# Two transformer blocks on one core: stage memory laid out from both ends of a partition, and one turn of the residual moved behind a group's last product

## The chip, the cores and the metric

One core of one Trainium2 chip. The metric is the time of one execution in microseconds (us) on the device, as the median of several runs; a lower time is better. A matrix product on TensorE multiplies a moving operand, streamed from on-chip memory (SBUF), by a stationary operand that was loaded from SBUF before, and adds into an accumulator bank (PSUM). SBUF has 128 partitions; every tile occupies the same bytes in each of them, so a tile's place is one byte offset. The offsets of this kernel run from 0 to 229376 (224 KiB).

## The reference

Two blocks on a residual `h` of 256 tokens x 1024 features, float32. Cut to its stages:

```python
# first block
z = rms_norm(x) @ w_in                       # differential attention, latent attention, two gates
x = x + rms_norm((sig(g_a) * (oa @ w_proj_a) + sig(g_b) * (ob @ w_proj_b)) @ w_o)
x = x + rms_norm((silu(n(x) @ w_gate) * (n(x) @ w_up)) @ w_down)
# second block, twice (i = 0: retention, i = 1: stick-breaking attention)
h = h + 0.5 * rms(swiglu(rms(h)))
h = h + rms(mixer(rms(h)))
h = h + 0.5 * rms(swiglu(rms(h)))
gate = sigmoid(rms(h) @ ple_w_gate[i])       # the gated embedding
e = p[i] @ ple_w_proj[i]
h = h + rms(gate * e)
```

## The kernel before

**Precision.** Each float32 matrix is split into a high and a low part of type float32r (`_hi`, `_lo`), and a product of two matrices is three products: hi by hi, hi by lo, lo by hi. `mm3` (lines 194 to 200) issues them in that order; all of them have line 197 in the profile. `mat_steps` (line 210; its products have line 214) is the other form, with the weights stationary and 256 tokens moving.

**Weights.** `chunk` (line 165) loads up to 2048 columns into `w_raw` (1 MB, one transfer on the SP queue), and splits them in pieces of 512 columns: ScalarE copies `w_hi` (line 188), VectorE subtracts for `w_lo` (line 189). There are 3 buffers of `w_raw` and 12 each of `w_hi` and `w_lo`.

**Stages.** In `tokens` (line 239) the stationary operand is a block of 128 tokens x 128 features of the stage's input, the moving operand 512 columns of weights. The input dimension is cut into groups; in each group token half b = 0 comes first, then b = 1, into separate PSUM banks. A feed-forward (`ffn`, line 612) runs six hidden blocks of gate and up this way with the stage input `x_hi`, `x_lo` stationary, turns each block's result `a` (transposes of line 628) and splits it into `a_hi`, `a_lo`, and then runs the down projection (`end_stage`, line 470) with `a_hi`, `a_lo` stationary. The mixers use the same forms with their own inputs: `oa`, `ob`, `m` in the first block, `u` for the retention's output, `o` for the stick-breaking output, `pe` for the embedding's projection.

**Stage joints.** At a stage's end `residual` (line 399) works for one token half: squares, a reciprocal root on GpSimd, and `h` is updated in two halves by VectorE (line 415). `features` (line 419) then turns the token half of `h`: eight transposes on TensorE (line 429, moving operand the identity in `kc`, stationary operand `h`), ScalarE makes `x_hi` (line 433), VectorE `x_lo` (line 435). It is called by the next stage's `tokens` as `before[b]`, ahead of that half's first products. Its transposes carry an order edge: they come, on TensorE, no earlier than the product kept in `self.turn_at`. `tokens` sets that name in every group and half at the product with `left == TURN_AT`, that is when 3 of the group's triples (9 products) are still to come. Turning half 0 thus stands among the last products of the stage before, turning half 1 among the products of half 0 in the first group. Within such edges the framework's scheduler orders the instructions of an engine by priority and by when it expects their inputs.

**The gated embedding** (`ple_gate`, line 1274) has two groups of the input dimension, 3 and 5 blocks. With two column parts that is 6 triples (18 products) per half in the first group and 10 triples (30 products) in the second. After the second group of a half follow tanh (`z`, line 1288), the product with `e` (line 1290), and `residual`. The next stage is the second layer's first feed-forward; after the second gated embedding the kernel ends.

**Memory.** All pools are stacked upwards from the start of SBUF in the order of their opening; pools that close give their place to the next. The bytes follow from the tile shapes and this order:

| pool or tile | bytes in a partition |
|---|---|
| descriptors and built-in constants | 0 to 16512 |
| `const` (with the identity `kc`), `raw` (3 x `w_raw`) | 16512 to 45024 |
| `hip` (`w_hi`), `lop` (`w_lo`) | 45024 to 69600, to 94176 |
| `act`: `h`; `x_hi`, `x_lo` (also `ob`) | 94176 to 102368; 102368 to 118752 |
| `sm`, `tmp` | 118752 to 136320 |
| first block: `oa`; `m` | 148608 to 164992; 164992 to 181376 |
| first block: `cq`, `ckv` | 194688 to 204928 |
| first feed-forward: `a_hi`, `a_lo` (22528 each) | 136320 to 181376 |
| `p_halves` (`pe`), open from here on | 136320 to 140416 |
| feed-forward ahead of each mixer: `a_hi`, `a_lo` | 140416 to 185472 |
| retention: `u_h`, `u_l` | 140416 to 173184 |
| stick-breaking: `o_h`, `o_l` | 152192 to 168576 |
| `emb` (`e`); feed-forward behind it: `a_hi`, `a_lo` | 140416 to 148608; 148608 to 193664 |

Of the kernel before, what the change touches and what calls it, by code (L numbers as in the profile page):

```python
# [10 lines left out]
F32 = mybir.dt.float32  # L11
# [7 lines left out]
P = 128  # L19
T = 256  # L20
D = 1024
KT = D // P
# [28 lines left out]
TURN_AT = 3  # L51
# [43 lines left out]
class Weights:  # L95


    def __init__(self):
        self.parts = []
# [45 lines left out]
class Build:  # L145
    def __init__(self, ctx, tc, aps):
        self.ctx, self.tc, self.nc = ctx, tc, tc.nc
        self.aps = aps
        self.plan = []
        self.at = 0  # L150
        pool = lambda name, bufs, **k: ctx.enter_context(tc.tile_pool(name=name, bufs=bufs, **k))
        self.const = pool("const", 1)
        self.raw = pool("raw", 3)
        self.hip = pool("hip", WB)
        self.lop = pool("lop", WB)
        self.act = pool("act", 1)
        self.sm = pool("sm", 2)
        self.tmp = pool("tmp", 2)
        self.psm = pool("psm", 4, space=PSUM)
        self.psa = pool("psa", 4, space=PSUM)  # L160
        self.filler, self.behind, self.late = Filler(), None, []
        self.later = None
# [73 lines left out]
        return ps  # L236


    def tokens(self, parts, X, nk, banks, groups, before=(None, None)):

        per = CHUNK // len(parts[0][2])
        for g in groups:
            at, order = {}, [(j, k) for j in range(len(parts)) for k in g]
            for i in range(0, len(order), per):
                part = order[i : i + per]
                W = self.chunk([(*parts[j][:2], k, parts[j][2]) for j, k in part])
                at.update({jk: (W, x * len(parts[0][2])) for x, jk in enumerate(part)})
            for b in range(2):  # L250
                if g is groups[0] and before[b] is not None:
                    before[b]()
                left = len(parts) * len(g)
                for j, (*_, cols) in enumerate(parts):
                    for k in g:
                        left -= 1
                        W, c = at[j, k]
                        x = tuple(t[:, k, b * P : (b + 1) * P] for t in X)
                        self.mm3(banks[b][j], x, W(c, len(cols)), k == groups[0][0], k == groups[-1][-1])
                        if left == TURN_AT:  # L260
                            self.turn_at = self.behind
                yield b, g is groups[-1]

# [236 lines left out]

    def setup(self):
        nc, const, aps = self.nc, self.const, self.aps
        self.h = self.act.tile([P, 2, D], F32, name="h", tag="h")

        self.h0 = self.h.rearrange("p b d -> p (b d)").rearrange("p (k t) -> p k t", k=KT)
        self.vecs = const.tile([P, NV], F32, name="vecs")
        self.kc = const.tile([P, NK], F32, name="kc")
        nc.scalar.dma_start(self.kc[:, :P], aps["kc"][:, :P])
        nc.scalar.dma_start(self.vecs[:, :KT], aps["vecs"][:, :KT])
        self.pos = self.tmp.tile([P, T], I32, name="pos", tag="s")  # L510
        self.lam = self.tmp.tile([P, 4 * 64], F32, name="lam", tag="s")
        self.ident = self.kc[:, K_ID : K_ID + P]
        self.ones = const.tile([P, P], F32, name="ones")
        nc.vector.memset(self.ones, 1.0)
        self.dummies(WARM[0])
        self.mhalf = const.tile([P, 2], F32, name="mhalf")
        nc.vector.memset(self.mhalf, -0.5)
# [756 lines left out]
    def ple_gate(self, i, X, R, before, e, row, out):  # L1274
        nc = self.nc
        gains = self.gain_row(row)
        parts = [("ple_w_gate_2", (i,), range(j * 512, (j + 1) * 512)) for j in range(2)]
        banks = self.banks(self.psm, "m")
        groups = [list(range(0, 3)), list(range(3, 8))]
        for b, done in self.tokens(parts, X, KT, banks, groups, before):  # L1280
            self.settle()
            if not done:
                continue
            with self.urgent():
                ys = []
                for j, c0, n in PIECES[b if out is not None else 0]:
                    z = self.ends.tile([P, 512], F32, name="z", tag="z", bufs=2)[:, :n]
                    nc.scalar.activation(z, banks[b][j][:, c0 : c0 + n], AF.Tanh, scale=R[:, b : b + 1])
                    eb = e[:, b, j * 512 + c0 : j * 512 + c0 + n]
                    nc.vector.scalar_tensor_tensor(eb, z, 1.0, eb, op0=ALU.add, op1=ALU.mult)  # L1290
                    ys.append(eb)
            self.residual(b, ys, gains, 1.0, 2.0, out)


    def run(self):
        tc = self.tc
        self.setup()
        g2 = lambda i, n: self.vec(V_G2 + (i * 8 + n) * 8, 8)
        row = lambda i, n: R_G2 + 4 * i + n // 2
        stage = self.first()  # L1300
        with tc.tile_pool(name="big0", bufs=1) as self.big:
            self.ffn(*stage, ("w_ffn_gate", "w_ffn_up", "w_ffn_down"), (0,), R_FFN, 1.0)
        names = ("ffn_w_gate_2", "ffn_w_up_2", "ffn_w_down_2")
        out = self.aps["out"].rearrange("p (b d) -> p b d", b=2)
        p_halves = self.ctx.enter_context(tc.tile_pool(name="p_halves", bufs=1))
        self.pe = [p_halves.tile([P, SUB], F32R, name=f"pe_{x}") for x in "hl"]
        pos = self.tmp.tile([P, T], I32, name="pos", tag="s")
        self.nc.gpsimd.dma_start(pos, self.aps["pos2"].to_broadcast([P, T]))
        self.table2 = self.rope_table("2", pos, self.kc[:, K_F2 : K_F2 + 1], self.const)
        for i in range(2):  # L1310
            with tc.tile_pool(name=f"big{i}a", bufs=1) as self.big:
                self.ffn(*self.next_stage(g2(i, 0)), names, (i, 0), row(i, 1), 4.0)
            self.later = lambda i=i: self.embed_in(i)
            mixer = self.stick if i else self.retention
            mixer(*self.next_stage(g2(i, 2)), row(i, 3))
            with tc.tile_pool(name=f"emb{i}", bufs=1) as emb:
                e = emb.tile([P, 2, D], F32, name="e")
                self.embed(i, e)
                with tc.tile_pool(name=f"big{i}b", bufs=1) as self.big:
                    self.ffn(*self.next_stage(g2(i, 4)), names, (i, 1), row(i, 5), 4.0)  # L1320
                self.ple(i, *self.next_stage(g2(i, 6), 4.0), e, row(i, 7), out if i else None)
        assert self.at == WCOLS * P, (self.at, WCOLS * P)
# [66 lines left out]
```

## Time and profile before

| | us |
|---|---|
| median of 3 runs | 1613.9 (1613.33 to 1614.34) |
| the profiled execution, its own time | 1613.39 |
| its span, first to last instruction | 1611.5 |
| TensorE busy with products | 1597.7 (99%) |
| VectorE busy | 1065.2 (66%) |
| ScalarE busy | 904.1 (56%) |
| GpSimd busy | 79.9 (5%) |

Read it as follows. The busy time of a product in the profile is longer than its share of TensorE's time, since products overlap: a 128x512 product shows some 390 ns, while the next begins 227 to 238 ns after it. So the time that a product costs is read from start to start, or from a run of products as its time over its count. The chain of waits does this: it goes back from the last instruction to what released each, and merges neighbours of one kind into a piece with a count.

### The profile page before, as it was taken

The page shows a single profiled execution, that of the slowest core. Times are in us where ns is not written, and L with a number is a line of the kernel's source. Part 1 is how long each engine was busy: PE and PEld are TensorE (multiplying, and loading weights), DVE is VectorE, ACT ScalarE, POOL GpSimd, SP SyncE. Part 2 cuts the span into 40 slices and gives each one's busy share as a digit, 9 for nine tenths or more (in the row PEclk, how much of TensorE's full clock was granted, in tenths as well). Part 3 has the DMA queues.
Part 4 walks back from the last instruction along what each step waited for, and adds up shares of the span by engine and source line. Part 5 has one row for each costly group of instructions (what it writes and reads, how often), then busy time and mean ns, then how long its engine had stood idle before and what let it go on. Part 6 is the DMA issues. An engine that isn't in the chain of part 4 may idle for free.

```text
span 1611.5 us, 22515 instructions
## 1 busy us (share of the span) xinstructions
PE 1597.7 (99%) x8230; PEld 1344.3 (83%) x8230; DVE 1065.2 (66%) x1969; ACT 904.1 (56%) x1792; POOL 79.9 (5%) x97
## 2 busy tenths in 40 slices
PE   9999999999999999999999999999999999999997
PEld 8898778888888888898888888878888899888886
DVE  7987766765566665777766555486665677666546
ACT  6665544755455554645546555476554656655545
POOL 0000000200001000100000000012000200000001
PEclk9999999999999999999999999999999999999999
DMA  7535436455546555555455555555555554455552
GB/s 243 211 123 190 167 106 221 183 179 201 183 159 220 183 183 183 167 189 183 160 190 179 187 178 188 183 198 200 183 183 183 176 192 149 165 183 183 183 175 73
DMA packets 47134, 288.72 MB, mean 179 GB/s; under 512 B 5968, under 2 KB 9168, under 8 KB 14384
## 3 DMA queue, kind: packets, MB, share of 16 engines
q1 hardware_dynamic: 44528, 279.29, 49.3%
q0 software_dynamic: 2064, 7.80, 1.4%
q8 instruction: 64, 1.05, 0.3%
q14 instruction: 46, 0.38, 0.1%
q10 hardware_dynamic: 432, 0.20, 0.0%
HBM read 284.78 MB, written 1.05 MB: 177 GB/s over the span
## 4 chain that ended last, share of the span: by engine, by line
PE 95%; DVE 2%; DMA 1%; issue 1%; ACT 1%; SPq 0%; POOL 0%; POOLq 0%; DVEq 0%; ACTq 0%
PE ps L197 78%; PE ps L214 9%; PE at L628 1%; PE S L660 1%; PE xt L429 1%; DMA w_raw<-in_w 1%; DVE w_lo L189 1%; PE o L197 1%; PE o L707 0%; DMA h<-in_x 0%; PE S L1073 0%; PE S L1187 0%; PE pt L697 0%; PE o L834 0%; PE ot L1110 0%
## 5 line engine op out<-in xcount | busy, mean ns | idle before, releaser
L189 DVE TENSOR_TENSOR w_lo<-w_raw,w_hi 128x512 fp32r<-128x512 f32 x1054 | 708.8, 687 | 348.8 <-ACT w_hi L188 343.5
L188 ACT CAST w_hi<-w_raw 128x512 fp32r<-128x512 f32 x1054 | 639.6, 621 | 489.2 <-PE ps L197 355.8
L197 PE MATMUL ps<-w_hi,x_hi 128*128 128x512 f32 (+1 forms) x1280 | 488.9, 382 | 0.3 <-ACT x_hi L433 0.3
L197 PE MATMUL ps<-w_hi,x_lo 128*128 128x512 f32 (+1 forms) x1280 | 483.0, 377 | 0.5 <-DVE x_lo L435 0.5
L197 PE MATMUL ps<-w_lo,x_hi 128*128 128x512 f32 (+1 forms) x1280 | 482.1, 377 | 0.0
L197 PEld LDWEIGHTS ps<-w_hi,x_lo 128*128 128x128 f32 x1280 | 240.8, 188 | 46.9 <-DVE x_lo L435 2.1
L197 PEld LDWEIGHTS ps<-w_hi,x_hi 128*128 128x128 f32 x1280 | 241.0, 188 | 43.3 <-issue 1.0
L197 PEld LDWEIGHTS ps<-w_lo,x_hi 128*128 128x128 f32 x1280 | 241.2, 188 | 42.1
L197 PE MATMUL ps<-w_hi,a_hi 128*128 128x512 f32 x440 | 176.7, 402 | 0.0
L197 PE MATMUL ps<-w_hi,a_lo 128*128 128x512 f32 x440 | 173.3, 394 | 0.0
L197 PE MATMUL ps<-w_lo,a_hi 128*128 128x512 f32 x440 | 172.6, 392 | 0.0
L296 POOL TENSOR_TENSOR r<-v,mhalf 128x1 f32<-128x1 f32 (+1 forms) x50 | 61.4, 1228 | 1262.6 <-DVE v L384 1097.7
L214 PE MATMUL ps<-x_hi,w_hi 128*128 128x256 f32 x440 | 114.8, 289 | 0.7 <-ACT x_hi L356 0.5
L214 PE MATMUL ps<-x_hi,w_lo 128*128 128x256 f32 x440 | 112.5, 284 | 0.6 <-DVE w_lo L189 0.6
L197 PEld LDWEIGHTS ps<-w_hi,a_lo 128*128 128x128 f32 x440 | 82.6, 188 | 21.3
L197 PEld LDWEIGHTS ps<-w_lo,a_hi 128*128 128x128 f32 x440 | 82.7, 188 | 19.2
L197 PEld LDWEIGHTS ps<-w_hi,a_hi 128*128 128x128 f32 x440 | 82.6, 188 | 18.4
L214 PEld LDWEIGHTS ps<-x_hi,w_hi 128*128 128x128 f32 x440 | 84.0, 191 | 2.2 <-issue 0.7
L214 PEld LDWEIGHTS ps<-x_hi,w_lo 128*128 128x128 f32 x440 | 84.1, 191 | 1.5 <-DVE w_lo L189 1.2
L623 DVE SCALAR_TENSOR_TENSOR a<-ps,R,s 128x512 f32<-128x512 f32 (+1 forms) x60 | 42.2, 703 | 55.4 <-PE ps L197 44.0
L214 PE MATMUL ps<-x_lo,w_hi 128*128 128x256 f32 x440 | 77.4, 283 | 0.0
L270 ACT CAST a_hi<-at 128x512 fp32r<-128x512 f32 (+1 forms) x60 | 33.1, 551 | 70.4 <-PE at L628 70.4
(271 smaller groups left out, 1484.0 us busy)
## 6 DMA issues: line engine op xcount, KB each, us to landing
w_raw<-in_w SPq DMA_DIRECT2D x254, 1024.0 KB, 4.9
gr<-in_rows POOLq DMA_DIRECT2D x10, 512.0 KB, 4.1
w_raw<-in_w SPq DMA_DIRECT2D x7, 512.0 KB, 3.4
w_raw<-in_w SPq DMA_DIRECT2D x12, 256.0 KB, 5.1
w_raw<-in_w SPq DMA_DIRECT2D x6, 384.0 KB, 3.3
h<-in_x SPq DMA_DIRECT2D x4, 256.0 KB, 5.6
h<-in_x POOLq DMA_DIRECT2D x1, 1024.0 KB, 8.9
out<-h SPq DMA_DIRECT2D x3, 256.0 KB, 2.5
```

Source lines behind the costliest of these rows:

```text
L188: nc.scalar.copy(hi[:, :m], r[:, c0:c1])
L189: nc.vector.tensor_sub(lo[:, :m], r[:, c0:c1], hi[:, :m].bitcast(F32))
L197: mm = lambda a, b, **k: nc.tensor.matmul(ps, a, b, skip_group_check=True, **k)
L214: mm = lambda *a, **k: self.nc.tensor.matmul(*a, skip_group_check=True, **k)
L270: nc.scalar.copy(hi, src)
L296: self.nc.gpsimd.tensor_tensor(r, v, self.mhalf[:, :n], op=ALU.pow)
L429: nc.tensor.transpose(pt[:, i, :], self.h[:, b, k * P : (k + 1) * P], self.ident)
L623: nc.vector.scalar_tensor_tensor(a, banks[1], R[:, b : b + 1], s, op0=ALU.mult, op1=ALU.mult)
L628: nc.tensor.transpose(pt[:, i, :], a[:, i * P : (i + 1) * P], self.ident)
L660: mm(S[:, at], q[:, qs], k[:, ks], start=n == 0, stop=n == len(parts[0]) - 1, skip_group_check=True)
```

## The change

It has two parts.

1. SBUF pools open on two sides. `hip`, `lop`, `act` and the pools of the stages stay on the left, stacked upwards; `const`, `raw`, `sm`, `tmp`, `p_halves`, `emb` and a new pool `res` that takes `h` out of `act` go to the right, stacked down from the upper end. By the shapes the left stack then has `w_hi` and `w_lo` at 16512 to 65664, `x_hi` and `x_lo` at 65664 to 82048, and every stage's pools from 82048 upwards; the right stack reaches down to 162816 when all of it is open. The sizes and the number of buffers are as before, and no instruction is added or removed.
2. `tokens` takes the value at which it sets `turn_at` as an argument. The default is the old value, 3; `ple_gate` gives 0, that is the last product of a group and half.

```diff
-        self.const = pool("const", 1)
-        self.raw = pool("raw", 3)
+        self.const = pool("const", 1, side="right")
+        self.raw = pool("raw", 3, side="right")
         self.hip = pool("hip", WB)
         self.lop = pool("lop", WB)
         self.act = pool("act", 1)
-        self.sm = pool("sm", 2)
-        self.tmp = pool("tmp", 2)
+        self.res = pool("res", 1, side="right")
+        self.sm = pool("sm", 2, side="right")
+        self.tmp = pool("tmp", 2, side="right")
...
-    def tokens(self, parts, X, nk, banks, groups, before=(None, None)):
+    def tokens(self, parts, X, nk, banks, groups, before=(None, None), turn_at=TURN_AT):
...
-                        if left == TURN_AT:
+                        if left == turn_at:
                             self.turn_at = self.behind
...
-        self.h = self.act.tile([P, 2, D], F32, name="h", tag="h")
+        self.h = self.res.tile([P, 2, D], F32, name="h", tag="h")
...
-        for b, done in self.tokens(parts, X, KT, banks, groups, before):
+        for b, done in self.tokens(parts, X, KT, banks, groups, before, 0):
...
-        p_halves = self.ctx.enter_context(tc.tile_pool(name="p_halves", bufs=1))
+        p_halves = self.ctx.enter_context(tc.tile_pool(name="p_halves", bufs=1, side="right"))
...
-            with tc.tile_pool(name=f"emb{i}", bufs=1) as emb:
+            with tc.tile_pool(name=f"emb{i}", bufs=1, side="right") as emb:
```

## Rows read from the trace of the kernel before

**Rows 1.** The page: TensorE's busy time, and the chain that ended last by engine.
```profile
PE 1597.7 (99%) x8230; PEld 1344.3 (83%) x8230; DVE 1065.2 (66%) x1969; ACT 904.1 (56%) x1792; POOL 79.9 (5%) x97
...
PE 95%; DVE 2%; DMA 1%; issue 1%; ACT 1%; SPq 0%; POOL 0%; POOLq 0%; DVEq 0%; ACTq 0%
```

**Rows 2.** Busy time by stretch: a down projection, a gate/up stage; then clock, DMA, GB/s.
```profile
418.00:474.00 56.00, 56.00 (x242) 45.06 (x241) 27.97 (x42) 25.99 (x44) 0.55 (x1) 1.00 0.54 188
384.00:402.00 18.00, 18.00 (x81) 14.87 (x80) 10.34 (x15) 9.71 (x16) 0.00 (x0) 1.00 0.61 213
```

**Rows 3.** Chain of waits (start, length in us, what), gate/up of the first feed-forward.
```profile
380.10 2.78 PE ps L197 x12
...
383.31 19.10 PE ps L197 x84
```

**Rows 4.** Chain of waits, the first feed-forward's down projection; the long piece occurs five times.
```profile
415.00 2.79 PE ps L197 x12
...
418.01 56.70 PE ps L197 x243
```

**Rows 5.** Chain of waits: w_o; retention's output and embedding; last mixer's output and embedding.
```profile
268.11 17.50 PE ps L197 x75
...
821.08 48.06 PE ps L197 x206
...
1371.96 17.06 PE ps L197 x73
```

**Rows 6.** TensorE in time order: first and last of 33 products on ob.
```profile
246.89 0.39 PE L197 MATMUL ps<-w_hi,ob_hi 128*128 128x512 f32 x1
...
254.15 0.39 PE L197 MATMUL ps<-w_hi,ob_lo 128*128 128x512 f32 x1
```

**Rows 7.** Groups by line and shape on VectorE: count, busy us, mean ns.
```profile
L189 DVE TENSOR_TENSOR w_lo<-w_raw,w_hi 128x512 fp32r<-128x512 f32 x1042 | 702.7, 689 | 348.2 <-ACT w_hi L188 342.9
...
L271 DVE TENSOR_TENSOR pe_l<-pt,pe_h 128x512 fp32r<-128x512 f32 x2 | 1.4, 688 | 1.0 <-ACT pe_h L270 1.0
```

**Rows 8.** Chain of waits: 256-wide products on cq and ckv, on x; transposes of a, h.
```profile
208.47 1.41 PE ps L214 x12
...
1352.56 1.43 PE ps L214 x12
...
360.13 0.44 PE at L628 x4
...
474.71 0.87 PE xt L429 x8
```

**Rows 9.** TensorE in time order, first gated embedding, the turn of half 1.
```profile
1063.12 0.39 PE L197 MATMUL ps<-w_lo,x_hi 128*128 128x512 f32 x1
1063.46 0.63 PE L429 MATMUL xt<-kc,h 128*128 128x128 f32 x4
...
1065.30 0.40 PE L197 MATMUL ps<-w_hi,x_hi 128*128 128x512 f32 x1
```

**Rows 10.** TensorE in time order, from the first gated embedding to the next feed-forward.
```profile
1080.79 0.39 PE L197 MATMUL ps<-w_hi,x_lo 128*128 128x512 f32 x1
1081.66 0.66 PE L429 MATMUL xt<-kc,h 128*128 128x128 f32 x4 [0.48 <-DVE h L415]
...
1084.46 0.40 PE L197 MATMUL ps<-w_hi,x_lo 128*128 128x512 f32 x1
1085.14 0.50 PE L197 MATMUL ps<-w_hi,x_hi 128*128 128x512 f32 x1 [0.29 <-ACT x_hi L433]
...
1086.89 0.50 PE L197 MATMUL ps<-w_hi,x_lo 128*128 128x512 f32 x1 [0.55 <-DVE x_lo L435]
...
1089.03 0.66 PE L429 MATMUL xt<-kc,h 128*128 128x128 f32 x4
```

**Rows 11.** VectorE and ScalarE in time order, the same stretch.
```profile
1080.86 1.42 DVE L415 SCALAR_TENSOR_TENSOR h<-og,r,h 128x512 f32<-128x512 f32 x2 [0.44 <-POOL r L296]
...
1084.73 0.36 ACT L433 ACTIVATE x_hi<-xt,vecs 128x128 fp32r<-128x128 f32 x1
```

## Prediction

> **What bounds the kernel now.** I read the page first: TensorE's matmuls are busy 1597.7 of 1611.5 us, and the chain that ended last is TensorE for 95% of the span [rows 1]. Neither the copies into buffers nor the loads end it: in a down projection and in a gate/up stage alike VectorE and ScalarE are busy about half of the time and the DMA engines 54 and 61%, at a granted clock of 1.00, the 2.4 GHz level [rows 2]. So nothing that only relieves these engines counts. Two things do: how long TensorE needs from one product to the next, and the few places where it waits.
>
> For the first I read the chain of waits, because it merges an unbroken run of products into one row, and its time over its count is the pace. The same instruction (line 197, 128x512, stationary and moving operand both in SBUF) has two paces. In the gate/up stages 84 products take 19.10 us, 227.4 ns each [rows 3]; in all five down projections 243 products take 56.70 us, 233.3 ns [rows 4]. Three other runs have 233.3 as well: 75 products of w_o in 17.50 us, 206 of the retention's output and of the embedding behind it in 48.06 us, and 73 of the last mixer's output and the second embedding in 17.06 us (233.7) [rows 5]. One run outside the gate/up stages is quick: line 197 with ob as the stationary operand, 33 products of which the first starts at 246.89 and the last at 254.15, 226.9 ns each [rows 6].
>
> What tells them apart? Not the code: ob runs through the same steps as the slow first half of the retention's output, and w_o through the same `tokens` as the quick gate/up. Not the work beside them [rows 2]. It is where the stationary operand lies, by the table in the section on the kernel before: x and ob occupy bytes 102368 to 118752 of a partition and are quick; w_o's m, the down projections' a, the outputs' u and o and the embedding's pe all begin at 136320 or above and are slow. The moving weights lie at 45024 to 94176 for all. Byte 131072, half of the 256 KiB of addresses, lies between the two groups; the trace can't say more exactly where the border is.
>
> A second thing is needed for the sum. Behind every burst of transposes even quick operands start slowly: 12 products of a gate/up stage right behind one take 2.78 us, 231.7 ns each [rows 3], as many of a down projection 2.79 us [rows 4]. So there is nothing to win in about the first 10 products behind a burst.
>
> **Part 1, the places.** The change adds and removes no instruction here. By the shapes, the left stack becomes hip (16512), lop (41088), x_hi and x_lo (65664 to 82048) and then each stage's own pools from 82048 up. So a_hi and a_lo come to 82048 to 127104 in all five feed-forwards, u to 82048 to 114816, o to 93824 to 110208, m to 110720 to 127104: all below 131072. Only pe stays above it (p_halves goes right). If place sets the pace, each of these products goes from 233.3 to 226.9 ns, 6.4 less:
> - down projections: 5 x (243 - 10) x 6.4 ns = 7.5 us
> - retention's output: 187 of the 206 have u, (187 - 5) x 6.4 ns = 1.2 us
> - w_o: (75 - 10) x 6.4 ns = 0.4 us
> - last mixer's output: 54 of the 73 have o, (54 - 10) x 6.4 ns = 0.3 us
> - runs of six between attention steps (oa, some of o): inside the slow start, nothing.
>
> That is 9.4 us. Its bounds: 0, if place is not the cause; 9.8, if the slow start costs no product its gain ((1215 + 187 + 75 + 54) x 6.4 ns).
>
> One part of it has no row: nothing stationary lies between 118752 and 136320 now, but a_lo from its 15th block of 22 (118784 up) and m_l (118912 up) will. If the border were at 118752, 8 of 22 blocks of each down projection keep the slow pace: 8/22 x 7.5 + 0.4 = 3.1 us of the gain are lost. I take the full gain, since 131072 is the only round border in that gap.
>
> What goes up to the right is read by other engines. VectorE's weight remainder takes 689 ns with all operands low, and the same form with its output and one input at 136320 and above (pe_l) 688 [rows 7]: no difference, and the engine has slack. TensorE reads three things on the right: the identity as moving operand, h as stationary operand of the transposes, and the embedding's halves, as before. Transposes cost 0.11 us each both with the stationary operand high (4 in 0.44) and low (8 in 0.87); a moving operand above the border costs nothing where there is one: 12 products of 256 columns moving cq and ckv take 1.41 us, 12 moving x 1.43 [rows 8]. So the 160 transposes of h (144 in `features`, 16 in `prenorm`) get 0, with ends from -0.3 us (0.02/12 ns each) to +1.0 us (6.4 ns each).
>
> Waits for reused memory: relative to each other the stage pools stay as they were, except that e and pe leave their stack. Nobody waits for the memory of e now, so there is nothing to win or lose; gr's loads on the POOL queue still reuse a's memory in the gated embedding and are issued as before. I put this at 0, with 0.5 us to either side for a different order of instructions.
>
> **Part 2, the turn behind the last product.** `turn_at` 0 in `ple_gate` acts at three places; no instruction is added.
>
> The first two are the turn of token half 1 at the start of each gated embedding. Now the transposes stand behind product 14 of 18, in two bursts: product 14 starts at 1063.12, the first product of the other half at 1065.30 [rows 9]. These 2.18 us hold 5 products (1.13) and 8 transposes (0.87), so 0.18 is lost. After: product 18 ends its turn at 1064.25, h is long there, the transposes end at 1065.12, and then x_hi has to be made with no product left to cover it; the first x_hi follows the first four transposes (1064.69) by some 0.6 us. First product at about 1065.3: no change, 0.3 us either way for each of two.
>
> The third is the end of the first gated embedding, where the next feed-forward's first turn stands. Now TensorE comes to the turn with 9 products left: it issues a product at 1080.79 and waits until 1081.66 for h, which VectorE begins to write only at 1080.86; after the 9 products, the last of which starts at 1084.46, it waits for x_hi (first product at 1085.14, because ScalarE converts weights before it begins x_hi at 1084.73), then for x_lo, until 1086.89; the turn of half 1 is at 1089.03 [rows 10, 11]. With the turn behind the last product the 9 run through from 1081.02 to 1083.06. By then all of h is written (1080.86 + 1.42), the transposes end at 1083.93, x_hi's first block takes ScalarE to about 1084.2, so the next stage starts 0.9 us sooner. What is late next is half 1's residual, which hangs on the last product: that ends 1.6 us sooner (1083.06 against 1084.69), and so does its chain to the turn at 1089.03; the 14 products between fit. I take 1.5 us, the smaller of the two for what the stage as a whole gains, with ends 0 (ScalarE's and VectorE's queues take the weights first again) and 2.2 us, all the waits there. Where the cover is gone the price is x_hi's 0.6 us, already in it.
>
> **Sum.** 9.4 + 1.5 = 10.9 us off the profiled execution's 1613.4 (span 1611.5 and 1.9 around it): 1602.5; the median of the runs is 0.5 higher: **1603.0 us**.
>
> **Rivals.**
> (a) Place counts only partly (a border at 118752, above): 1603.0 + 3.1 = 1606.1, with the turn giving nothing 1607.6.
> (b) Place is not the cause, and the slow stages have some other thing in common. Then only the turn is left: 1613.9 - 1.5 = 1612.4, no measurable difference. For it: m, a, u and o are all made inside their stage, from transposed or attended values, and x is not. Against it: ob is made so too, and it is quick [rows 6]. The Trainium skill's page "SBUF — State Buffer", section "Who interferes with whom", speaks for this rival: it says that TensorE has read ports of its own and that "PE and ACT never wait on anyone"; it names no price for where in a partition an operand lies. The rows disagree with that as a full account: 227 against 233 ns for one form.
> (c) Slower. Quick is not "below a border" but the band in which the stationary operand lies now, or its distance from the moving one. x moves from 102368 to 65664, where no 512-wide stationary operand has been, and the weights to 16512. Then the gate/up stages lose their quick pace: each feed-forward has five runs like those of 84, 25 in all, x 74 products behind the slow start x 6.4 ns = 11.8 us, and part 1 brings nothing: 1613.9 + 11.8 - 1.5 = 1624.2. It ends on the slower side as soon as it takes more than the turn's 1.5 us, which 4 of the 25 runs do; should part 1 bring its 9.4 all the same, 23 of them. Against it: the 256-wide products of line 214 have stationary weights from 45024 up and moving x above them, the other way round, and their pace (1.43 us for 12) is no worse than with other places [rows 8].
>
> **How the numbers follow.** Forecast 0.72, (a) 0.10, (b) 0.11, (c) 0.07. The forecast's own range: the largest gain is 9.8 + 2.2 + 0.6 (the two first turns) + 0.3 (transposes) + 0.5 (order) = 13.4, the smallest 9.4 - 0.6 - 1.0 - 0.5 = 7.3, so 1600.5 to 1606.6. Reaching to (a) at 1607.6, and with the 1.0 us by which the runs of before differ on both sides, the range is 1599.5 to 1608.6; it leaves out (b) and (c), 0.18. A measurement tells 0.2% (3.2 us) from no change: faster 0.82, same 0.11, slower 0.07.
>
> **What would show it.** In the chain of waits of the changed kernel the five rows of 243 products should read about 55.2 us instead of 56.70, the gate/up rows still 19.10; w_o's 75 about 17.1. At the end of the first gated embedding one burst of eight transposes should follow the last product with no wait before it. Gate/up rows near 19.6 would be (c); rows of 56.7 with the turn done (b); rows near 55.7 (a).

## The result and the profile after

The changed kernel takes 1603.54 us (median of four runs, 1602.18 to 1605.17) against 1613.73 us of the kernel before beside it (1613.33 to 1614.34): a ratio of 0.9937, 95% interval 0.9920 to 0.9954. Its profiled execution takes 1602.92 us, with a span of 1600.8 us.

From the page of the changed kernel, the busy time of its engines and the chain that ended last:

```profile
PE 1586.2 (99%) x8230; PEld 1345.8 (84%) x8230; DVE 1063.6 (66%) x1969; ACT 904.7 (57%) x1792; POOL 88.0 (5%) x97
...
PE 95%; DMA 2%; DVE 1%; ACT 1%; issue 1%; SPq 0%; POOL 0%; POOLq 0%; DVEq 0%; ACTq 0%
```

TensorE still is the bound, with the share it had [rows 1]. What changed is its pace. The chain of waits of the changed kernel (start, length in us, engine, tile, line, count; lines below `features` are 2 higher than before), w_o, gate/up and down projection of the first feed-forward, retention's output with its embedding, the last mixer's output with its embedding:

```profile
267.88 17.03 PE ps L199 x75
...
359.78 19.08 PE ps L199 x84
...
417.14 55.13 PE ps L199 x243
...
816.58 46.88 PE ps L199 x206
...
1363.18 16.78 PE ps L199 x73
```

Against [rows 3 to 5]: gate/up was 19.10 and is 19.08; the down projection's 243 products go from 56.70 to 55.13 (226.9 ns each, five times), w_o from 17.50 to 17.03, the 206 products from 48.06 to 46.88, the 73 from 17.06 to 16.78. These rows give 5 x 1.57 + 0.47 + 1.18 + 0.28 = 9.78 us, nearly all that there is: TensorE's last product starts 10.73 us sooner.

At the end of the first gated embedding the turn stands behind the last product. Rows picked from TensorE, VectorE and ScalarE in time order, to be held against [rows 10, 11]:

```profile
1075.41 0.40 PE L199 MATMUL ps<-w_hi,x_lo 128*128 128x512 f32 x1
1075.64 1.04 PE L431 MATMUL xt<-kc,h 128*128 128x128 f32 x8
1075.96 0.69 DVE L414 TENSOR_TENSOR og<-e,gr 128x512 f32<-128x512 f32 x1
1076.57 0.69 DVE L191 TENSOR_TENSOR w_lo<-w_raw,w_hi 128x512 fp32r<-128x512 f32 x1
1076.68 1.13 ACT L435 ACTIVATE x_hi<-xt,vecs 128x128 fp32r<-128x128 f32 x4
1077.09 0.50 PE L199 MATMUL ps<-w_hi,x_hi 128*128 128x512 f32 x1 [0.41 <-ACT x_hi L435]
1077.17 0.69 DVE L1292 SCALAR_TENSOR_TENSOR e<-z,e 128x512 f32<-128x512 f32 x1
1077.77 0.69 DVE L191 TENSOR_TENSOR w_lo<-w_raw,w_hi 128x512 fp32r<-128x512 f32 x1
1078.37 0.69 DVE L414 TENSOR_TENSOR og<-e,gr 128x512 f32<-128x512 f32 x1
1079.10 0.34 DVE L437 SCALAR_TENSOR_TENSOR x_lo<-xt,vecs,x_hi 128x128 fp32r<-128x128 f32 x1
1079.50 0.50 PE L199 MATMUL ps<-w_hi,x_lo 128*128 128x512 f32 x1 [1.21 <-DVE x_lo L437]
1080.65 1.32 PE L431 MATMUL xt<-kc,h 128*128 128x128 f32 x8
```

One burst of eight transposes follows the last product without a wait for h, and x_hi comes 0.41 us late. But VectorE has four steps of the other half's residual and of the weights ahead of x_lo (the rows at 1076.57 to 1078.37), and TensorE waits 1.21 us for it. The stretch from the last transposes of `a` ahead of the gated embedding to the first ones of the next feed-forward holds one down projection and this joint. The kernel before takes 108.68 us for it and the changed one 107.31; the quicker down projection alone is 1.57, so the turn has brought nothing.

### The profile page after: what moved, and what is told of

Read it like the earlier page. It is cut to its first block, busy times and chain, and to the rows that moved or that the text cites. A ratio compares the mean times of both kernels' runs of the same rounds, so it can differ in the third digit from the quotient of the medians.

```text
span 1600.8 us, 22511 instructions
## 1 busy us (share of the span) xinstructions
PE 1586.2 (99%) x8230; PEld 1345.8 (84%) x8230; DVE 1063.6 (66%) x1969; ACT 904.7 (57%) x1792; POOL 88.0 (5%) x97
## 4 chain that ended last, share of the span: by engine, by line
PE 95%; DMA 2%; DVE 1%; ACT 1%; issue 1%; SPq 0%; POOL 0%; POOLq 0%; DVEq 0%; ACTq 0%
PE ps L199 78%; PE ps L216 10%; DMA w_raw<-in_w 2%; PE at L630 2%; PE S L662 1%; PE xt L431 1%; PE o L199 1%; PE o L709 0%; DVE w_lo L191 0%; ACT w_hi L190 0%; PE S L1075 0%; PE S L1189 0%; PE pt L699 0%; PE o L836 0%; PE ot L1112 0%
## 5 line engine op out<-in xcount | busy, mean ns | idle before, releaser
L199 PE MATMUL ps<-w_hi,a_hi 128*128 128x512 f32 x440 | 172.8, 393 | 0.0
L298 POOL TENSOR_TENSOR r<-v,mhalf 128x1 f32<-128x1 f32 (+1 forms) x50 | 69.9, 1403 | 1243.1 <-DVE v L386 1077.6
```

What stands on the lines that cost most here:

```text
L199: mm = lambda a, b, **k: nc.tensor.matmul(ps, a, b, skip_group_check=True, **k)
L298: self.nc.gpsimd.tensor_tensor(r, v, self.mhalf[:, :n], op=ALU.pow)
```

## The experiments

**The two parts alone.** The first has the pools of the change and the old turn; the second the old pools and the new turn.

```diff
-        self.const = pool("const", 1)
-        self.raw = pool("raw", 3)
+        self.const = pool("const", 1, side="right")
+        self.raw = pool("raw", 3, side="right")
...
```

> Part 1 alone: the pools on two sides, the turn where it was before. Theory A (the whole gain is the stationary operand's place, the turn brings nothing): 10.7 us below the kernel before, as the whole change; the rows of 243 products 55.2 us, and the wait for h at the end of the first gated embedding (0.6 us ahead of the transposes) is back. Rival (the turn has its forecast 1.5 us): 9.2 us below the kernel before, 1.5 us above the whole change.

Measured: 1602.2 us, ratio 0.9928 (0.9916 to 0.9941). The whole gain is part 1; the stretch above takes 107.14 us with the old turn.

```diff
...
-        for b, done in self.tokens(parts, X, KT, banks, groups, before):
+        for b, done in self.tokens(parts, X, KT, banks, groups, before, 0):
```

> Part 2 alone: the pools as before, the turn behind the last product in the gated embedding. Theory A: 0 +- 0.4 us against the kernel before, because TensorE then waits for x_lo in place of h. Rival: 1.5 us faster. The rows of 243 products stay at 56.70 us under both.

Measured: 1614.34 us, ratio 1.0002 (0.9993 to 1.0011); rows of 243 still 56.70. The turn in time order (line numbers as before):

```profile
1083.02 1.03 PE L429 MATMUL xt<-kc,h 128*128 128x128 f32 x8
...
1084.46 0.50 PE L197 MATMUL ps<-w_hi,x_hi 128*128 128x512 f32 x1 [0.41 <-ACT x_hi L433]
...
1086.87 0.50 PE L197 MATMUL ps<-w_hi,x_lo 128*128 128x512 f32 x1 [1.19 <-DVE x_lo L435]
```

The first x_hi product starts at 1084.46 instead of 1085.14, four such products run, and then the first x_lo product starts at 1086.87, as before at 1086.89 [rows 10]. (Some 0.1 us of the difference is not the turn's: the burst of transposes at the start of the gated embedding already came at 1057.07 instead of 1057.18.) What the turn gained, the wait for x_lo took back.

**Is it a border at 131072?** In the changed kernel x goes high (184448 to 200832), or the weights go high (w_hi 200832, w_lo 176256).

```diff
-        self.act = pool("act", 1)
+        self.act = pool("act", 1, side="right")
```

> The changed kernel with the pool of x_hi, x_lo and ob on the right (x_hi at 184448, x_lo at 192640); a, u, o and m stay low. Theory A (place of the stationary operand): the gate/up rows of 84 products go from 19.10 to about 19.57 us (74 x 6.4 ns more), 25 such rows and the other x runs cost some 15 us, so about 1618, slower than the kernel before; the rows of 243 stay at 55.2. Rival (something that the stages of a, u, o and m share, not the place): gate/up rows stay at 19.10 and the time at 1603.

```diff
-        self.raw = pool("raw", 3, side="right")
-        self.hip = pool("hip", WB)
-        self.lop = pool("lop", WB)
+        self.raw = pool("raw", 3)
+        self.hip = pool("hip", WB, side="right")
+        self.lop = pool("lop", WB, side="right")
```

> The changed kernel with the weights' pools w_hi and w_lo on the right (176256 to 225408) and w_raw on the left instead: in the tokens form the moving operand is high and the stationary one low, in the form of line 216 the stationary one is high. Theory A (only the stationary operand's place counts): rows of 243 at 55.2 and gate/up rows at 19.10 as in the changed kernel; the 256-wide products with stationary weights go from 120 to about 126 ns, 1320 of them, 8 us more: 1611. Rival B (the two operands' places count as a pair, a high moving operand helps as in the 117.5 ns of cq and ckv): 512-wide products lose 2 to 3 ns each, 5300 of them, 13 us: about 1598 to 1600 after the 8 us for line 216. Rival C (any high operand costs): rows of 243 at 56.70, gate/up rows at 19.57, about 1635.

Measured: 1602.98 us (ratio 0.9930) and 1603.07 us (0.9933). A gate/up row with x high, and a down projection's with the weights high:

```profile
360.82 19.08 PE ps L199 x84
```

```profile
417.27 55.13 PE ps L199 x243
```

Stationary operands above 131072 are quick here. The border of the prediction is refuted, though pe, at 170976 in the changed kernel, 154592 and 146400 in these two, stayed slow in all of them. With the weights high none of the three expected times came (1611, 1598 to 1600, 1635): the products with stationary weights, which were to lose 6 ns, kept their median of 120 ns. The next theory was a band of slow places, between about 131072 and some 181000.

**A band?** x at 158688 to 175072 in the changed kernel; pe low in the changed kernel; the kernel before with only the feed-forwards' pools on the right, so that a lies at 176096 to 221152; and a across 131072 by an unused tile ahead of it.

```diff
-        self.act = pool("act", 1)
...
+        self.act = pool("act", 1, side="right")
```

> The changed kernel with x (x_hi 158688, x_lo 166880) put on the right side below h and the temporaries, instead of at 65664; every stage pool moves down by 16384 bytes. With x at 184448 the gate/up products had kept their quick pace, so a border at 131072 alone is refuted; what is left of the place theory is a band. Band theory: what is stationary between about 131072 and 181000 is slow. Then the gate/up runs of 84 products read 19.6 us instead of 19.08, about 3360 products x 6.4 ns = up to 21 us come on top, and the kernel is at about 1620 to 1624. Theory that it is not the absolute place of the stationary operand: rows of 84 stay at 19.08, kernel at 1603.

```diff
-        p_halves = self.ctx.enter_context(tc.tile_pool(name="p_halves", bufs=1, side="right"))
+        p_halves = self.ctx.enter_context(tc.tile_pool(name="p_halves", bufs=1))
```

> The changed kernel with p_halves left on the left side: pe_h and pe_l lie at 82048 to 86144 instead of 170976, and all other stage operands move up by 4096. In every kernel so far the 24 products of each embedding on pe have been slow (median 232 to 234 ns), with pe at 136320, 146400, 154592 and 170976. Band theory: pe now takes 227 ns, 48 x 7 ns = 0.3 us less, and the chain's run of u and pe (206 products) becomes 46.8 us. Theory that pe is slow for another reason: it stays at 234. The time of the kernel is about 1603 in both.

```diff
...
-            with tc.tile_pool(name=f"big{i}a", bufs=1) as self.big:
+            with tc.tile_pool(name=f"big{i}a", bufs=1, side="right") as self.big:
...
```

> The kernel before with one edit: the feed-forwards' own pools go to the right side, so a_hi lies at 176096 to 198624 and a_lo at 198624 to 221152, instead of at 136320 to 181376 or 148608 to 193664. Weights, x, u, m, o, h, the constants and the temporaries stay where they were. Theory that all above 131072 is slow, or that a has to be near the weights: rows of 243 products stay at 56.7 us, kernel at 1614. Band theory (slow only up to about 181000): rows of 243 become 55.1, kernel faster by 1215 x 6.4 ns = 7.8 us, about 1606; u, m and o stay slow.

```diff
+        pad = self.big.tile([P, 4096], F32, name="pad", tag="pad")
+        nc.gpsimd.memset(pad[:, 0:1], 0.0)
```

> The changed kernel with 16384 unused bytes ahead of the feed-forwards' own tiles, so a_hi lies at 98432 to 120960 and a_lo at 120960 to 143488: its blocks 0 to 9 below 131072, 10 to 21 above. Nothing else moves. Border at 131072: in each down projection the products of blocks with a_lo above the border turn slow, and as a quick run takes some ten products to be quick again after a slow one, the groups from block 10 up are slow altogether: rows of 243 about 55.9 us, kernel about 1606.5. Border at 118752: slow all through, 56.7 us, kernel at 1611. No border here: rows at 55.13, kernel at 1603.

Measured: x in the band 1625.12 us (ratio 1.0071, 1.0056 to 1.0086); pe low 1602.90 (0.9932); a high in the old layout 1605.51 (0.9948, 0.9933 to 0.9963); a across 131072 1603.52 (0.9938). The chains of waits: x in the band (a gate/up row, a down projection), then a high in the old layout (w_o, gate/up, down projection), then a across 131072:

```profile
364.90 19.67 PE ps L199 x84
...
423.41 55.14 PE ps L199 x243
```

```profile
268.57 17.51 PE ps L197 x75
...
361.01 19.10 PE ps L197 x84
...
418.42 55.13 PE ps L197 x243
```

```profile
417.97 55.13 PE ps L199 x243
```

All four came out as a band would have it, if its lower end is put above `a`'s 143488 in the fourth. (The fourth expectation has some ten products slow behind a slow one; the kernel before has four there: behind the last product on `a`, at 477.53, those on x take 236, 228, 233 and 230 ns from start to start, and then 227.) In the third, `a` alone is moved and `a` alone turns quick; w_o stays at 17.51. So the place of the stationary operand is the cause, but what about the place? The layouts offered a second reading that fits every row as well: the remainder of the addresses by 64. In the kernel before, the weights (45024) and x (102368) have remainder 32, all stage operands 0; a at 176096 has 32 and is quick. In the changed kernel the weights (16512), x and the stage operands have 0 and only pe has 32; x at 158688 has 32 and is slow.

**Remainder or band?** 32 unused bytes settle it: in the kernel before, ahead of the stage pools; in the changed one, ahead of x.

```diff
+        pad = self.sm.tile([P, 8], F32, name="pad", tag="pad", bufs=1)
+        nc.gpsimd.memset(pad, 0.0)
```

> The kernel before with 32 unused bytes put among the small tiles, ahead of the temporaries: every stage pool moves up by 32 bytes (a_hi from 136320 to 136352, u, m, o, oa and pe likewise), the weights and x stay. In all eight kernels so far the quick products are those whose stationary and moving operand have addresses with the same remainder by 64, the slow ones those where the remainders differ by 32; before, the weights and x have remainder 32, all stage operands 0. Theory of the common remainder by 64: a, u, m and pe turn quick at their old place, rows of 243 read 55.1 us, and the kernel takes the whole gain, about 1603. If the remainder by 128 counts, nothing changes yet (the differences become 64): 1614. Theory of a band of slow places from some 144000 to 175000: nothing changes, 1614.

```diff
+        pad = self.act.tile([P, 8], F32, name="pad", tag="pad")
+        nc.gpsimd.memset(pad, 0.0)
```

> The changed kernel with 32 unused bytes ahead of x: x and every operand in the stage pools move up by 32 bytes, the weights stay at 16512. Theory of the common remainder: now all stationary operands differ from the weights by 32; the gate/up rows of 84 read 19.6 us, the rows of 243 56.7, and the kernel loses what x lost at 158688 (about 21 us) and the gain of the change (about 10 us): about 1634. Theory of a band of slow places: all of it lies below 130000, nothing changes, 1603.

Measured: 1606.25 us (ratio 0.9958, 0.9944 to 0.9972) and 1627.15 us (1.0087, 1.0074 to 1.0101). The chain of the kernel before with 32 bytes (w_o, gate/up, down projection), then that of the changed kernel with 32 bytes (gate/up, its last block with 256 columns, down projection):

```profile
267.23 17.18 PE ps L197 x75
...
359.40 19.10 PE ps L197 x84
...
416.84 55.62 PE ps L197 x243
```

```profile
384.79 19.59 PE ps L199 x84
...
408.09 8.52 PE ps L199 x72
...
419.86 56.69 PE ps L199 x243
```

The band falls: 32 bytes make `a` quicker at its old place, and make x and `a` slow where they were quick, far below the band. The stationary operand's own remainder does not decide it either: `a` stands at 128 by 256 in the kernel before (136320), where it is slow, and in the changed kernel (82048), where it is quick. What differs is the weights' remainder by 256, 224 and 128. But the remainder by 64 is not the whole rule: 55.62 us is 228.9 ns a product, neither 226.9 nor 233.3. There the distance from the weights is a multiple of 64, not of 128.

**Which remainder, and the wait for x_lo.** In one kernel x_lo goes ahead of the other half's residual at the end of the first gated embedding, and 32 bytes shift pe. In the last one each kind of operand has its own distance.

```diff
-        with self.urgent():
+        with self.tc.high_priority(ahead):
...
-                self.ffn(*self.next_stage(g2(i, 0)), names, (i, 0), row(i, 1), 4.0)
+                self.ffn(*self.next_stage(g2(i, 0), ahead=400 if i else 100), names, (i, 0), row(i, 1), 4.0)
...
+        pad = self.sm.tile([P, 8], F32, name="pad", tag="pad", bufs=1)
```

> The changed kernel with two small edits: at the end of the first gated embedding x_hi and x_lo of token half 0 go ahead of the other half's residual on ScalarE and VectorE, and 32 unused bytes among the small tiles bring pe to the weights' remainder by 64. If the wait for x_lo behind the 8 transposes is what took back the gain of the turn, TensorE's wait of 1.21 us for x_lo there goes, and the stage starts up to 1.2 us sooner, unless the residual of half 1, which is then made later by some 2 us, takes it back at its own turn. pe's 48 products take 0.3 us less by the theory of the common remainder. Together about 1602, or 1603.2 if the residual takes the turn's part back.

Measured: 1601.23 us (ratio 0.9928, 0.9915 to 0.9940), the lowest median of all, though its interval meets those of the changed kernel and of part 1 alone. VectorE and TensorE in time order:

```profile
1075.38 1.03 PE L431 MATMUL xt<-kc,h 128*128 128x128 f32 x8
...
1078.12 2.15 DVE L437 SCALAR_TENSOR_TENSOR x_lo<-xt,vecs,x_hi 128x128 fp32r<-128x128 f32 x8
1078.52 0.51 PE L199 MATMUL ps<-w_hi,x_lo 128*128 128x512 f32 x1 [0.49 <-DVE x_lo L437]
```

The wait is 0.49 us instead of 1.21, half 1's turn doesn't wait for h, and the stretch from transposes to transposes takes 106.22 us instead of 107.31. Against the 107.14 us of the old turn in the same layout that is 0.9 us, of the 1.5 that the turn was to bring. The 32 bytes gave pe nothing: it stayed at 234 ns, with a remainder by 64 of 0 (the median of its products from start to start). So the expectation for pe was wrong, and the period had to be looked for once more.

```diff
+        self.gap(self.act, 32, "pad0")
+        self.halves()
+        self.gap(self.act, 32, "pad1")
+        self.gap(self.sm, 104, "pad2", bufs=1)
...
+        self.gap(self.big, 32, "pad3")
```

> The changed kernel with unused bytes that give each kind of stationary operand its own distance from the weights: counted as address of the stationary minus address of the moving operand, remainder by 512, x has 128, u, m and o 256, a 384, pe 448 (0, 0, 0 and 352 in the changed kernel). So far: remainder 0 took 226.8 ns a product, 32 and 160 233.3, 192 228.9, 320 and 352 234.4. If a period of 128 bytes were the rule, 0, 192 and 320 would not all differ as 0 and 64 by 128 do, so it is not the whole rule; x, u and a quick here would still be in its favour (kernel at 1603). With a period of 256: u, m and o quick (rows of 75 at 17.1 us), x (rows of 84) and a (rows of 243) at some pace of their own, pe at 192's 229 ns. With 512: u, m and o slow too. Bounds of the time: 1603 with all quick, 1603 + 21 + 10 = 1634 with all at 233 to 234.

Measured: 1625.64 us (ratio 1.0080, 1.0063 to 1.0096). Its chain: w_o, gate/up, down projection, retention's output with the embedding:

```profile
268.98 17.02 PE ps L199 x75
...
362.46 19.59 PE ps L199 x84
...
420.80 56.46 PE ps L199 x243
...
827.01 46.76 PE ps L199 x206
```

m and u, at a remainder of 256 by 512, are as quick as at 0; x and a, at 128 and 384, are slow. pe shows its pace in the run of 206, which is 187 products of u and 19 of pe. Beside the 46.76 above, the same row with pe low, and in the kernel with x_lo first:

```profile
817.38 46.72 PE ps L199 x206
```

```profile
816.35 46.85 PE ps L199 x206
```

With pe low all 206 are quick, 226.8 ns each. The 0.13 and 0.04 us more are 7 and 2 ns for each of 19 products of pe: 234 and 229. The medians of all products on pe from start to start say the same: 227, 234 and 229 ns. For every run of 512-column products that is long enough to leave the slow start behind, the pace then goes by one number, the address of the stationary minus that of the moving operand, remainder by 256:

| remainder | ns a product | from |
|---|---|---|
| 0 | 226.9 | 55.13 / 243 (changed kernel, a); 17.02 / 75 (last kernel, m, distance 256) |
| 32 | 233.3 | 56.69 / 243 (a, 32 bytes in the changed kernel) |
| 64 | 234 | pe, x_lo first |
| 96 | 234.2 | 19.67 / 84 (x at 158688) |
| 128 | 232.3, 233.2 | 56.46 / 243 (a), 19.59 / 84 (x), last kernel |
| 160 | 233.3 | [rows 4] |
| 192 | 228.9 | 55.62 / 243 (a, 32 bytes in the kernel before); pe 229, last kernel |

A remainder of 224 was not run. That 256 and 0 agree, and 448 and 192, while 128 and 0 do not, makes 256 the period. Two limits remain. At 128 the two rows differ: behind their first 15 products x (128 by 512) takes 233.0 ns and `a` (384) 232.4, and no run says why. And the weights stood at two remainders by 256 only, 224 and 128; that it is the difference of the two addresses rests on its being 0 in the quick rows of both.

The slow pace is not even. In the down projections before, TensorE in time order:

```profile
430.45 0.40 PE L197 MATMUL ps<-w_hi,a_hi 128*128 128x512 f32 x1
430.69 0.39 PE L197 MATMUL ps<-w_lo,a_hi 128*128 128x512 f32 x1
430.92 0.39 PE L197 MATMUL ps<-w_hi,a_lo 128*128 128x512 f32 x1
431.15 0.40 PE L197 MATMUL ps<-w_hi,a_hi 128*128 128x512 f32 x1
```

The product of w_hi and a_hi takes 238 ns from start to start, the other two 231, again and again. What VectorE and ScalarE do does not make this: the 370 of these products during which neither VectorE nor ScalarE was busy took the same, 237.8, 230.9 and 231.3 ns.

## Why the prediction was right, and where it was not

**The sizes held.** The rows of 243 were to read about 55.2 and read 55.13; gate/up was to stay and did. By the terms: down projections 7.85 us against 7.5, retention's output 1.18 against 1.2, w_o 0.47 against 0.4, the last mixer's output 0.28 against 0.3. Together it is the upper bound of 9.8, because the step of 6.4 ns was too small. The 226.9 ns of ob has its slow start in it; behind the first 15 products of a run, the two paces are 233.33 and 226.67 ns, 6.7 apart. The first ten were not quite without gain either: in the down projections they went from 233.6 to 231.2 ns. The products on these and three smaller operands outside the four kinds of row, counted at nothing, gave 1.1 us more.

**The cause failed.** The step that failed is the one after "What tells them apart?": two groups of places were found, and the one round number between them was taken for the cause. With x at 184448 it fell. The same table of places holds the right answer: x lies 57344 bytes from w_hi, 224 x 256; a lies 91296 from it, 356 x 256 + 160. "The moving weights lie at 45024 to 94176 for all" was read as a reason to leave them out, though half of the cause is there. That the number came out right is luck: the new stacks happen to satisfy both rules. On the left stand only tiles whose sizes are multiples of 512 bytes, so that all distances are multiples of 256, while before the pool of small tiles, in slots of 32 bytes, lay between the weights and the stage pools. The right-hand side itself does nothing, as x and the weights on the right show; pe, below the small tiles there, is the one operand that the change left slow.

**The rivals.** (a), a border at 118752, falls with `a` across it at 55.13. (b), that place is not the cause, falls with `a` alone moved in the old layout. Its support was the Trainium skill's page "SBUF — State Buffer", section "Who interferes with whom": TensorE never waits on anyone. As to VectorE and ScalarE the traces agree with this, by the 370 products above; what differs between 227 and 233 ns is the distance of TensorE's own two operands. (c) named the distance from the moving operand, rightly, but as a size. It was a real danger: with 32 bytes more on the left the change would have been slower, 1627 us.

**The turn failed.** Its first half happened as worked out: the nine products run through, and the next stage's first product starts 0.68 us sooner, some 0.6 of it by the turn (0.9 was said). The failing term is "I take 1.5 us": of its two ends the lower one, that "ScalarE's and VectorE's queues take the weights first again", was true of VectorE, and x_lo, not the residual of half 1, is late next. (Of the "14 products between" the trace of before has 12.) The two first turns brought nothing, as said. The missing 1.5 us were made up for by the long rows (0.4) and the short runs (1.1), which was luck too: 10.9 us were predicted for the profiled executions, 10.5 came.

**A test that agreed with the wrong theory.** x at 158688 gave 1625 us where the band expected 1620 to 1624. It moved place and remainder at once; only the 32 bytes moved one without the other.

## What to carry to other kernels

When one form of instruction has two paces, list for both the addresses of all its operands, and their differences by small powers of two, before taking a large border for the cause. Here TensorE's stationary and moving operand wanted a distance that is a multiple of 256 bytes; 32 bytes of padding are a cheap experiment. A gain from a moved pool should be tested by padding, because what moved may be only the remainder.

## What was not expected of the hardware

The two operands' distance costs up to 7.3 ns of 226.9 in a product of 512 columns, 3%, with the weight loads at a mean of 188 or 189 ns in slow and quick runs alike; the clock is no part of it, its granted mean is 0.998 or 0.999 in the three kernels with x slow, and 0.997 to 0.999 in those with x quick. Products of 256 columns don't follow the same order: the 72 on x in a feed-forward's last gate/up block take 8.52 us at remainder 32, and in the changed kernel, at 0, the row below. That is 118.3 against 119.9 ns, and it is most of why 32 bytes cost the changed kernel 24 us and not the 31 that were expected: its 1956 products of 256 columns with a weight as one operand, from start to start and with their waits, took 4.9 us less.

```profile
405.31 8.63 PE ps L199 x72
```

Why the remainder matters, why the first ten or so products behind transposes, and the first four behind slow ones, are slow even at remainder 0, and what a remainder of 224 gives, stays open; no run tells it.
